# Gates of both token halves together, and four smaller edits, in a two-layer trunk on one core

## The chip, the cores and the metric

The program runs on one core of a Trainium2 chip. The metric is the device time of one execution in microseconds (us); three runs of the kernel before gave 1740.96, 1741.60 and 1741.65, median 1741.6. TensorE (PE) multiplies; PEld is its weight load; VectorE is DVE, ScalarE is ACT, GpSimd is POOL, and SyncE (SP) issues most DMAs.

## The reference

`x` is 1024 tokens by 1024 features in float32, `c` one vector that conditions every sub-layer through scale, shift and gate. Two layers; the change lies in the first, whose mixer is recurrent:

```python
for i in range(DEPTH):                                   # 2 layers
    mod = silu(c) @ w_mod[i] + b_mod[i]                  # six vectors of 1024
    sh_m, sc_m, gt_m, sh_f, sc_f, gt_f = split(mod, 6)
    h = rms_norm(x, norm_mix_g[i]) * (1 + sc_m) + sh_m
    y = recurrent_mixer(h) if i == 0 else pool_mixer(h)
    x = x + gt_m * y
    h = rms_norm(x, norm_ffn_g[i]) * (1 + sc_f) + sh_f
    x = x + gt_f * (square(relu(h @ w1)) @ w2)           # 4096 wide
return rms_norm(x, final_norm_g)

def recurrent_mixer(h):
    gate_branch = gelu(h @ w_y + b_y)
    xr = causal_depthwise_conv(h @ w_in + b_in)          # width 4
    r, g = sigmoid(xr @ w_a + b_a), sigmoid(xr @ w_x + b_x)   # 4 blocks of 256 x 256
    log_a = 8 * r * log_sigmoid(lam)
    a, u = exp(log_a), sqrt(-expm1(2 * log_a)) * (g * xr)
    s[t] = a[t] * s[t-1] + u[t]                          # scan over tokens
    return (s * gate_branch) @ w_out + b_out
```

## The kernel before

Features lie on the 128 partitions, tokens along the free axis: `x` is eight blocks of 128 features, and the tokens are two halves of `H` = 512 (h = 0, 1). Float32 products are made of three fp32r matmuls of 512 columns: `mm3` (L184) multiplies high by high, high by low and low by high parts, and `proj` (L192) sums eight blocks, 24 matmuls. High parts are copies by ACT, low parts subtractions by DVE (`split_part`, L178), by POOL, or a DMA that adds (`neg_part`, L160).

Resources: six accumulators of PSUM for products (`acc_mm`), two for small ones (`small_ps`), 19 slots of 4 x 512 columns, seven temporaries, and three raw buffers (`rawp`) that weight loads and the conditioning's loads share. A product can't begin until an accumulator has been evicted.

The order on each engine is not the order of the text. A planner runs the program on its own costs when it is built, and gives a free engine the ready instruction that was written first; the engines then keep that order and wait for each other by semaphores. `tc.issue_after` and the helper `after` (L321) tie an instruction behind another one on its engine by hand.

The first layer goes as follows.

- Start (L102 to L402). Loads of `x`, of the modulation weights `mw` and of the projection's weights `w_k`. `s0` sums the squares of half 0: ACT squares a block, DVE adds it (`SumSq.add`, L252). `rstd_bcast` (L265) sums over partitions by small matmuls with a column of ones (L272), takes root and reciprocal, and spreads the result over all partitions by two fp32r matmuls with diagonals (L286), high and low part. `scale_of(k)` and `bias_of(k)` (L335, L338) make the modulation's columns on DVE. Then eight steps k normalize a block and multiply it into six accumulators `ps6` (L401).
- Between (L408 to L470). Half 1 of `x` is loaded, its squares are summed (`s1`, L443), the six accumulators are evicted with the bias (`conv_input`, L446), blocks 6 and 7 of half 0 are projected, half 1 is normalized and projected, and `conv` does the four taps.
- Gates (L502 to L565). For each of four heads, `split_unit` loads and splits a gate unit and two gelu units, and then for each half: `gates` (four gate products of six matmuls, sigmoids, Exp, Tanh, Sqrt, the scan) and two `gelu_block` (24 matmuls each). The scan writes over the convolution's output; Exp has a temporary `a`.

```python
    for hd in range(4):
        rate[0] = hd
        ...
        for h in range(2):
            gates(hd, ug, h)
            if (hd, h) == (3, 1):
                split_y(0)
            for mi in range(2):
                gelu_block(2 * hd + mi, uy[mi], h)
```

- Conditioning. The remaining 80 columns of the modulation (`mod_steps`, L216) are a 512 KB load `mb` and a DVE instruction (L207) each. `split_unit` and `f2_weights` call `drip(n)`, which issues n of them; n is `rate[0]` in the mixer and `DRIPS` (1 each) in the FFN. The first FFN's norm needs 24 of them, its end 32.
- First FFN (`f1(0, 0)`, L858): the norm of half 1 (`ffn_norm`) is made beside the first products of half 0.
- End (L1013 to L1038). The last products come in pieces: half 0, then the tokens of half 1 in two pieces of 256. `last_chunk` sums squares as they come; each letter of its plan names a sum, and equal letters are added on DVE. The last piece's sum is spread over the partitions before the root (`rstd_row`, L993), so that root and reciprocal take 128 x 256 elements.

## Time and profile before

| | |
|---|---|
| median of three runs | 1741.6 us |
| the profiled execution | 1740.4 us |
| its span, first to last instruction | 1738.5 us |
| mean granted clock of TensorE | 0.994 |
| PE busy | 1690.5 us (97%), 7472 matmuls |
| DVE, ACT, POOL busy | 1358.9, 967.2, 492.3 us (78, 56, 28%) |
| moved by DMA | 187.33 MB, mean 108 GB/s |

All times within the execution are from the span's start. A busy time is the union of an engine's instructions. Matmuls follow each other faster than each one lasts, so a busy PE may still run below its rate: the number of matmuls in a window tells more. The granted clock is 1.00 at 2.4 GHz and 0.50 at 1.2 GHz; a window with both shows a mean. Waits are put down to the instruction that came last by the profile.

### The profile page before, as it was taken

Reading aid. Unit: us, or ns where it says so; the run is one execution under the profiler, and the core shown is the slowest. Engines: PE = TensorE matmul, PEld = TensorE weight load, DVE = VectorE, ACT = ScalarE, POOL = GpSimd, SP = SyncE. Lnnn points to the kernel's source line nnn. Section 1 sums busy time; section 2 is a strip of 40 time slices with the busy share of each in tenths; the row PEclk is TensorE's granted clock in tenths of the full one; section 3 lists DMA queues with packets and bytes.
Section 4 is the critical chain, followed back from the end, with each engine's and each line's share of the span. In section 5 each row is a group of like instructions: output and inputs, shape, how many; then the busy total and the mean of one; then the engine's idle time right before and its main releaser. Section 6 shows DMA issues by size and latency. Waiting matters only on the chain.

```text
span 1738.5 us, 20871 instructions
## 1 busy us (share of the span) xinstructions
PE 1690.5 (97%) x7472; PEld 1386.7 (80%) x7472; DVE 1358.9 (78%) x2115; ACT 967.2 (56%) x1660; POOL 492.3 (28%) x419
## 2 busy tenths in 40 slices
PE   6899999999999999999999999999999999999997
PEld 4687778877788888888888888888878787878787
DVE  7897867589898989897973898559696868687847
ACT  6588886555454454545457787745444454545432
POOL 2132343103241414151416333303140405041403
PEclk9999999999999999999999999999999999999999
DMA  9423425642423333332319888841111112120202
GB/s 337 168 93 104 143 85 162 143 119 83 136 72 123 95 99 109 96 117 89 123 37 198 202 192 179 190 118 61 49 59 39 61 38 70 39 69 29 80 6 97
DMA packets 63175, 187.33 MB, mean 108 GB/s; under 512 B 6752, under 2 KB 9184, under 8 KB 63072
## 3 DMA queue, kind: packets, MB, share of 16 engines
q1 hardware_dynamic: 47376, 157.43, 27.6%
q0 software_dynamic: 15696, 28.58, 9.9%
q8 instruction: 58, 0.95, 0.2%
q14 instruction: 45, 0.37, 0.1%
HBM read 181.79 MB, written 4.19 MB: 107 GB/s over the span
## 4 chain that ended last, share of the span: by engine, by line
PE 75%; DVE 10%; issue 3%; ACT 3%; DMA 2%; POOL 1%; DVEq 0%; ACTq 0%; POOLq 0%
PE mm L188 25%; PE mm L189 25%; PE mm L190 25%; DMA mb<-in_wmod 2%; DVE mb L207 1%; DVE xa L773 1%; DVE xb L773 1%; POOL xa L782 1%; DVE xcb L440 1%; DVE w_a_s L181 1%; ACT c L777 0%; DVE gate L530 0%; PE sm L272 0%; DVE w_y L181 0%; DVE w_s L181 0%
## 5 line engine op out<-in xcount | busy, mean ns | idle before, releaser
L188 PE MATMUL mm<-hh,w_w 128*128 128x512 f32 x1024 | 399.7, 390 | 0.9 <-DVE xa L773 0.9
L189 PE MATMUL mm<-hl,w_w 128*128 128x512 f32 x1024 | 399.3, 390 | 0.0
L190 PE MATMUL mm<-hh,w_w 128*128 128x512 f32 x1024 | 399.0, 390 | 0.0
L782 POOL TENSOR_TENSOR xb<-xb,c 128x512 f32<-128x512 f32 x104 | 150.0, 1442 | 625.4 <-ACT c L777 625.2
L188 PEld LDWEIGHTS mm<-hh,w_w 128*128 128x128 f32 x1024 | 192.6, 188 | 43.1 <-DVE xa L773 3.0
L190 PEld LDWEIGHTS mm<-hh,w_w 128*128 128x128 f32 x1024 | 192.6, 188 | 40.2
L189 PEld LDWEIGHTS mm<-hl,w_w 128*128 128x128 f32 x1024 | 192.5, 188 | 39.5
L782 POOL TENSOR_TENSOR xa<-xa,c 128x512 f32<-128x512 f32 x104 | 159.7, 1535 | 145.2 <-ACT c L777 145.2
L777 ACT ACTIVATE c<-c,mod 128x512 f32<-128x512 f32 x104 | 75.3, 724 | 202.6 <-DVE c L803 135.5
L623 ACT ACTIVATE relu<-mm 128x512 f32<-128x512 f32 x128 | 76.2, 596 | 144.7 <-PE mm L190 144.7
L207 DVE SCALAR_TENSOR_TENSOR mb<-mb,cond 128x1024 f32<-128x1024 f32 x80 | 114.5, 1434 | 47.9 <-DMA mb<-in_wmod 47.9
L773 DVE SCALAR_TENSOR_TENSOR xa<-mm,mod,xa 128x512 f32<-128x512 f32 x156 | 113.0, 742 | 25.8 <-POOL xa L782 25.8
L181 DVE TENSOR_TENSOR w_w<-raw_w,w_w 128x512 fp32r<-128x512 f32 x112 | 106.8, 962 | 12.4 <-ACT w_w L180 12.4
L165 POOL DMA_DIRECT2D w_w<-in_w x80 | 70.5, 900 | 151.0 <-ACT w_w L164 120.6
L613 DVE TENSOR_TENSOR u<-usq,u 128x512 fp32r<-128x512 f32 x102 | 70.2, 688 | 16.1 <-ACT u L612 15.8
L188 PE MATMUL mm<-u,w_a_a 128*128 128x512 f32 x200 | 79.1, 396 | 2.3 <-DVE xb L773 1.2
L188 PE MATMUL mm<-u,w_w 128*128 128x512 f32 (+1 forms) x224 | 80.9, 361 | 0.0
L189 PE MATMUL mm<-u,w_w 128*128 128x512 f32 (+1 forms) x224 | 80.5, 360 | 0.1
L190 PE MATMUL mm<-u,w_w 128*128 128x512 f32 (+1 forms) x224 | 80.4, 359 | 0.0
L180 ACT CAST w_w<-raw_w 128x512 fp32r<-128x512 f32 x112 | 65.1, 612 | 25.0 <-PE mm L190 17.3
L189 PE MATMUL mm<-u,w_a_a 128*128 128x512 f32 x200 | 78.0, 390 | 0.0
L190 PE MATMUL mm<-u,w_a_a 128*128 128x512 f32 x200 | 77.9, 389 | 0.0
(326 smaller groups left out, 4030.0 us busy)
## 6 DMA issues: line engine op xcount, KB each, us to landing
raw_w<-in_w SPq DMA_DIRECT2D x148, 512.0 KB, 3.5
mb<-in_wmod SPq DMA_DIRECT2D x80, 512.0 KB, 3.8
w_w<-in_w POOLq DMA_DIRECT2D x80, 256.0 KB, 5.5
mw<-in_wmod SPq DMA_DIRECT2D x16, 512.0 KB, 11.0
raw_in<-in_w_in SPq DMA_DIRECT2D x8, 512.0 KB, 7.0
raw_y<-in_w_y SPq DMA_DIRECT2D x8, 512.0 KB, 3.7
raw_o<-in_w_out SPq DMA_DIRECT2D x8, 512.0 KB, 4.2
outT<-o SPq DMA_DIRECT2D x12, 256.0 KB, 2.2
```

The costliest lines, as they stand in the source:

```text
L165: nc.gpsimd.dma_start(w[:, 1, 0:n], src, accum_op=ALU.add)
L180: S.copy(w[:, 0, 0:n], raw)
L181: (eng or V).tensor_sub(w[:, 1, 0:n], raw, w[:, 0, 0:n].bitcast(F32))
L188: PE.matmul(out=ps, lhsT=wh, rhs=rh, start=first, stop=False)
L189: PE.matmul(out=ps, lhsT=wh, rhs=rl, start=False, stop=False)
L190: PE.matmul(out=ps, lhsT=w[:, 1, c:c + P], rhs=rh, start=False, stop=last)
L207: V.scalar_tensor_tensor(raw, raw, 1.0, cond, op0=ALU.mult, op1=ALU.mult, accum_out=m[:, e:e + 1])
L613: eng.tensor_sub(u[n][:, 1, jj, :], src, u[n][:, 0, jj, :].bitcast(F32))
L623: S.activation(r, ps, AF.Relu)
L773: V.scalar_tensor_tensor(xb, ps, g[:, r + 4 * row:r + 4 * row + 1], xb, op0=ALU.mult, op1=ALU.add)
L777: S.activation(t, src, AF.Identity, scale=g[:, r + 4 * row:r + 4 * row + 1])
L782: G.tensor_add(xb, xb, t)
```

## The change

Five edits.

- First norm: a class `ColumnSums` squares each block on ACT and adds over partitions and blocks on PE at once (four small matmuls a block, all accumulating in one PSUM tile); DVE's additions go. `rstd_bcast` gets a form `quick`: the diagonal in float32, one matmul, no high and low parts. DVE's `scale_of(0)` is now issued behind the norm's diagonal.
- Evictions: the six `conv_input` of half 0 are written before the squares of half 1.
- Gates: `gates` takes both halves of a head, function by function; half 0's sigmoids go to a slot, Exp and the scan write over the convolution's output, and the product of input gate and convolution is made before Exp. Then come the four gelu blocks; `split_y(0)` follows the last head.
- Conditioning: the rates of the four heads are 1, 2, 2, 3 instead of 0, 1, 2, 3, and the four units of the first FFN block take none.
- End: the last piece's plan is VVVVVXYZ instead of VVVVVVVX, and its norm is `rstd_bcast(..., quick=True)`; `rstd_row` goes. In `rstd_bcast` the loops over sums and quarters change places.

```diff
@@ -248,6 +248,7 @@
             self.name, self.n, self.plan, self.room = name, n, plan, room
             self.parts = {}
             self.i = 0
+            self.ps = None
         def add(self, xb):
             who = self.plan[self.i]
@@ -262,18 +263,43 @@
                 S.activation(sq, xb, AF.Square)
                 return (G if who == "G" else V).tensor_add(a, a, sq)
-    def rstd_bcast(ss, trace=None):
+    class ColumnSums:
+        def __init__(self, n=H):
+            self.n, self.parts, self.i, self.ps = n, {}, 0, small_ps()
+        def add(self, xb):
+            sq = tmp("sq", self.n)
+            S.activation(sq, xb, AF.Square)
+            for q in range(self.n // P):
+                PE.matmul(out=self.ps[:, q:q + 1], lhsT=sq[:, q * P:(q + 1) * P], rhs=ones[:, 0:1],
+                          start=(self.i == 0 and q == 0), stop=(self.i == NB - 1), skip_group_check=True)
+            self.i += 1
+    def rstd_bcast(ss, trace=None, quick=False):
         nq = ss.n // P
         parts = list(ss.parts.values())
-        ps = small_ps()
-        for q in range(nq):
+        ps = ss.ps
+        if ps is None:
+            ps = small_ps()
             for pi, a in enumerate(parts):
-                PE.matmul(out=ps[:, q:q + 1], lhsT=a[:, q * P:(q + 1) * P], rhs=ones[:, 0:1],
-                          start=(pi == 0), stop=(pi == len(parts) - 1))
+                for q in range(nq):
+                    PE.matmul(out=ps[:, q:q + 1], lhsT=a[:, q * P:(q + 1) * P], rhs=ones[:, 0:1],
+                              start=(pi == 0 and q == 0), stop=(pi == len(parts) - 1), skip_group_check=True)
         r = mp.tile([P, 4], F32, tag="rstd", name="rstd", bufs=2)
         root = S.activation(r[:, 0:nq], ps[:, 0:nq], AF.Sqrt, bias=eps, scale=1.0 / D)
         V.reciprocal(r[:, 0:nq], r[:, 0:nq])
+        if quick:
+            bc = small_ps()[:, 0:ss.n]
+            dg = tmp("dg", ss.n)
+            last = V.tensor_mul(dg.rearrange("p (q i) -> p q i", i=P), ident[:, None, :].to_broadcast([P, nq, P]),
+                                r[:, 0:nq, None].to_broadcast([P, nq, P]))
+            PE.matmul(out=bc, lhsT=ones, rhs=dg, start=True, stop=True)
+            if trace is not None:
+                trace[S], trace[V] = root, last
+            return bc
         rh = mp.tile([P, 4], F32R, tag="rstdh", name="rstdh", bufs=2)[:, 0:nq]
         V.tensor_copy(rh, r[:, 0:nq])
@@ -304,10 +330,10 @@
         hh[h] = Blocks(f"hh{h}", F32R)
         hl[h] = Blocks(f"hl{h}", F32R)
-    s0 = SumSq("m00", plan="VVVVVVVV")
+    s0 = ColumnSums()
     for k in range(NB):
         with tc.issue_after(cond_copy[k >= 6].ins) if k in (4, 6) else nullcontext():
-            last = s0.add(x[0][:, k, :])
+            s0.add(x[0][:, k, :])
     a, b = const.tile([P, NB], F32, name="amix0"), mod_tile(0, 0)
@@ -338,9 +364,8 @@
     def scale_of(k):
         column(a, 1, k, vcol("gmix0", k), b1[:, k:k + 1])
-    tail_of[V] = last
+    bc0 = rstd_bcast(s0, tail_of, quick=True)
     scale_of(0)
-    bc0 = rstd_bcast(s0, tail_of)
     parts = []
@@ -440,11 +465,11 @@
                 V.scalar_tensor_tensor(o, xr[:, k:k + H], vcol(f"cw{k}", m), o,
                                        op0=ALU.mult, op1=ALU.add)
+    xr = [conv_input(m, ps6[m], 0) for m in range(6)]
+    taken = last_traced(S)
     s1 = SumSq("m01", plan="VVVVVVVV")
     for k in range(NB):
         s1.add(x[1][:, k, :])
-    xr = [conv_input(m, ps6[m], 0) for m in range(6)]
-    taken = last_traced(S)
     xr.append(conv_input(6, proj(uin[6], hh[0], hl[0]), 0))
     bc1 = rstd_bcast(s1)
     xr.append(conv_input(7, proj(uin[7], hh[0], hl[0]), 0))
@@ -499,45 +524,51 @@
     behind.close()
-    def gates(hd, unit, h):
-        xchl = slot("xchl", (2, 2, H), F32R)
-        xch, xcl = xchl[:, 0, :, :], xchl[:, 1, :, :]
-        src = xc[h][:, 2 * hd:2 * hd + 2, :]
-        S.copy(xch, src)
-        V.tensor_sub(xcl, src, xch.bitcast(F32))
-        rs, gs = [], []
-        for mi in range(2):
-            b = 2 * hd + mi
-            for g in range(2):
-                ps = acc_mm()
-                for k in range(2):
-                    mm3(ps, unit, ((g * 2 + k) * 2 + mi) * P, xch[:, k, :], xcl[:, k, :], k == 0, k == 1)
-                t = tmp("gate")
-                S.activation(t, ps, AF.Sigmoid, bias=vcol("ba" if g == 0 else "bx", b))
-                (rs if g == 0 else gs).append(t)
-        aa = []
-        for mi in range(2):
-            b = 2 * hd + mi
-            av = tmp("a")
-            S.activation(av, rs[mi], AF.Exp, scale=coef[:, b:b + 1])
-            S.activation(rs[mi], rs[mi], AF.Tanh, scale=ncoef[:, b:b + 1])
-            aa.append(av)
-        for mi in range(2):
+    def gates(hd, unit, halves):
+        xchl, rs, gs = {}, {}, {}
+        for h in halves:
+            xchl[h] = slot("xchl", (2, 2, H), F32R)
+            src = xc[h][:, 2 * hd:2 * hd + 2, :]
+            S.copy(xchl[h][:, 0, :, :], src)
+            V.tensor_sub(xchl[h][:, 1, :, :], src, xchl[h][:, 0, :, :].bitcast(F32))
+        for h in halves:
+            room = slot("gates") if h == 0 else None
+            for mi in range(2):
+                b = 2 * hd + mi
+                for g in range(2):
+                    ps = acc_mm()
+                    for k in range(2):
+                        mm3(ps, unit, ((g * 2 + k) * 2 + mi) * P, xchl[h][:, 0, k, :], xchl[h][:, 1, k, :],
+                            k == 0, k == 1)
+                    t = tmp("gate") if room is None else room[:, 2 * mi + g, :]
+                    S.activation(t, ps, AF.Sigmoid, bias=vcol("ba" if g == 0 else "bx", b))
+                    (rs if g == 0 else gs)[h, mi] = t
+        both = [(h, mi) for h in halves for mi in range(2)]
+        hs = {(h, mi): xc[h][:, 2 * hd + mi, :] for h, mi in both}
+        for at in both:
+            G.tensor_mul(gs[at], gs[at], hs[at])
+        for at in both:
+            b = 2 * hd + at[1]
+            S.activation(hs[at], rs[at], AF.Exp, scale=coef[:, b:b + 1])
+            S.activation(rs[at], rs[at], AF.Tanh, scale=ncoef[:, b:b + 1])
+        for at in both:
             e = tmp("asq")
-            G.tensor_mul(e, aa[mi], aa[mi])
-            V.scalar_tensor_tensor(rs[mi], e, 1.0, rs[mi], op0=ALU.add, op1=ALU.mult)
-        for mi in range(2):
-            b = 2 * hd + mi
-            S.activation(rs[mi], rs[mi], AF.Sqrt)
-            hs = xc[h][:, b, :]
-            G.tensor_mul(gs[mi], gs[mi], hs)
-            V.tensor_mul(gs[mi], gs[mi], rs[mi])
-            V.tensor_tensor_scan(hs, aa[mi], gs[mi], 0.0 if h == 0 else carry[:, b:b + 1],
+            G.tensor_mul(e, hs[at], hs[at])
+            V.scalar_tensor_tensor(rs[at], e, 1.0, rs[at], op0=ALU.add, op1=ALU.mult)
+        for at in both:
+            h, b = at[0], 2 * hd + at[1]
+            S.activation(rs[at], rs[at], AF.Sqrt)
+            V.tensor_mul(gs[at], gs[at], rs[at])
+            V.tensor_tensor_scan(hs[at], hs[at], gs[at], 0.0 if h == 0 else carry[:, b:b + 1],
                                  op0=ALU.mult, op1=ALU.add)
             if h == 0:
-                V.tensor_copy(carry[:, b:b + 1], hs[:, H - 1:H])
+                V.tensor_copy(carry[:, b:b + 1], hs[at][:, H - 1:H])
     def gelu_block(m, unit, h):
         ps = proj(unit, hh[h], hl[h])
@@ -554,15 +585,14 @@
             V.tensor_sub(yl[h][:, k, :], xc[h][:, k, :], yh[h][:, k, :].bitcast(F32))
     for hd in range(4):
-        rate[0] = hd
+        rate[0] = (1, 2, 2, 3)[hd]
         ug = split_unit(w_g[hd], f"g{hd}")
         uy = [split_unit(w_y[m], f"y{m}") for m in (2 * hd, 2 * hd + 1)]
+        gates(hd, ug, (0, 1))
         for h in range(2):
-            gates(hd, ug, h)
-            if (hd, h) == (3, 1):
-                split_y(0)
             for mi in range(2):
                 gelu_block(2 * hd + mi, uy[mi], h)
+    split_y(0)
     wo = [split_unit(w_out[m], f"o{m}", G, 0) for m in range(4)]
     split_y(1)
@@ -680,7 +710,7 @@
     DRIPS = (1, 1, 1, 1, 1, 1, 1, 1)
     def f1_jobs(i, c, eng=None):
-        return [partial(lambda j: split_unit(w1[i, c * 4 + j], f"w1_{i}_{c}_{j}", eng, DRIPS[j]), j) for j in range(4)]
+        return [partial(lambda j: split_unit(w1[i, c * 4 + j], f"w1_{i}_{c}_{j}", eng, 0 if (i, c) == (0, 0) else DRIPS[j]), j) for j in range(4)]
     def f2_jobs(i, c, eng=None):
         return [partial(lambda r: f2_weights(i, c, r, eng), r) for r in range(4)]
@@ -990,17 +1020,6 @@
     osrc = outT.rearrange("(b p) t -> p b t", p=P)
     units = [split_unit(w2[1, 7, dp], f"w2_1_7_{dp}") for dp in range(4)]
-    def rstd_row(ss):
-        parts = list(ss.parts.values())
-        ps = small_ps()[:, 0:ss.n]
-        for pi, a in enumerate(parts):
-            PE.matmul(out=ps, lhsT=ones, rhs=a, start=(pi == 0), stop=(pi == len(parts) - 1))
-        r = tmp("rrow", ss.n)
-        S.activation(r, ps, AF.Sqrt, bias=eps, scale=1.0 / D)
-        V.reciprocal(r, r)
-        return r
     def final_norm(bc, h, t0, n):
         per = H // n
         for k0 in range(0, NB, per):
@@ -1034,8 +1053,8 @@
     n1 = 256
     sa = last_chunk(0, 0, H, "VVVVVVVV")
     sb = last_chunk(1, 0, n1, "VVVVVVVV", once(lambda: final_norm(rstd_bcast(sa), 0, 0, H)))
-    sc = last_chunk(1, n1, H - n1, "VVVVVVVX", mid_norm())
-    final_norm(rstd_row(sc), 1, n1, H - n1)
+    sc = last_chunk(1, n1, H - n1, "VVVVVXYZ", mid_norm())
+    final_norm(rstd_bcast(sc, quick=True), 1, n1, H - n1)
 def _layout(inputs):
```

## Rows read from the trace of the kernel before

**Rows 1.** The page's slices of PE: busy tenths in 40 equal slices.
```profile
PE   6899999999999999999999999999999999999997
```

**Rows 2.** Waits of PE, whole span: us in total, times, longest us.
```profile
PE mm L188 <- ACT gelu L545: 6.1, 4, 1.9
...
PE mm L188 <- ACT xr L426: 4.0, 1, 4.0
...
PE sm L272 <- DVE mod L210: 3.9, 1, 3.9
```

**Rows 3.** Windows of PE: window, length, busy us (matmuls), granted clock, DMA share, GB/s.
```profile
60.00:70.00 10.00, 8.17 (x26) 0.66 0.07 28
...
230.00:240.00 10.00, 8.13 (x29) 0.83 0.37 132
240.00:250.00 10.00, 10.00 (x45) 1.00 0.08 31
...
360.00:370.00 10.00, 6.76 (x27) 0.83 0.48 155
```

**Rows 4.** ACT by line, 122 to 253: count | busy us, mean ns | idle before, releaser.
```profile
L517 ACT ACTIVATE gate<-mm,vec 128x512 f32<-128x512 f32 x28 | 17.6, 691 | 0.2
L524 ACT ACTIVATE a<-gate,coef 128x512 f32<-128x512 f32 x14 | 9.4, 716 | 0.1
...
L517 ACT ACT_TABLE_LOAD x7 | 9.0, 1283 | 0.1
...
L533 ACT ACTIVATE gate<-gate 128x512 f32<-128x512 f32 x14 | 8.7, 632 | 12.1 <-DVE gate L530 12.0
```

**Rows 5.** Window of all engines, 122 to 253 (PE, PEld, DVE, ACT, POOL busy).
```profile
122.00:253.00 131.00, 124.88 (x541) 101.87 (x540) 106.56 (x153) 108.71 (x147) 44.53 (x30) 0.99 0.36 117
```

**Rows 6.** Conditioning's columns by line, 122 to 262, columns as in rows 4.
```profile
L207 DVE SCALAR_TENSOR_TENSOR mb<-mb,cond 128x1024 f32<-128x1024 f32 x18 | 26.5, 1475 | 11.2 <-DMA mb<-in_wmod 11.2
```

**Rows 7.** Timeline of DVE, 345 to 365: start, duration, instruction [idle before <- releaser].
```profile
358.83 1.23 DVE L207 SCALAR_TENSOR_TENSOR mb<-mb,cond 128x1024 f32<-128x1024 f32 x1 [2.08 <-DMA mb<-in_wmod]
...
361.26 1.23 DVE L207 SCALAR_TENSOR_TENSOR mb<-mb,cond 128x1024 f32<-128x1024 f32 x1 [0.59 <-DMA mb<-in_wmod]
...
362.41 0.69 DVE L263 TENSOR_TENSOR ssq<-ssq,sq 128x512 f32<-128x512 f32 x1
```

**Rows 8.** Timeline of PE, 3 to 21 and about 70.
```profile
4.17 3.78 PE L154 MATMUL sm<-dg,ones 128*128 128x512 f32 x4 [4.17 <-DVE dg L152]
11.96 1.87 PE L272 MATMUL sm<-ones,ssqm00V 128*128 128x1 f32 x8 [4.01 <-DVE ssqm00V L263]
...
18.66 2.08 PE L401 MATMUL mm<-hh,w_k 128*128 128x512 f32 x4 [1.86 <-ACT hh L328]
...
69.97 0.95 PE L272 MATMUL sm<-ones,ssqm01V 128*128 128x1 f32 x8
```

**Rows 9.** Timeline of DVE, 10 to 20 and 45 to 52.
```profile
11.82 1.34 DVE L328 CUSTOM_DVE_ANT_0 mw<-mw,cond,bmix 128x1024 f32<-128x1024 f32 x1
...
15.26 0.68 DVE L284 TENSOR_TENSOR dg<-ident,rstd 128x512 fp32r<-128x512 f32 x1
...
47.20 1.34 DVE L328 CUSTOM_DVE_ANT_0 mw<-mw,cond,bmix 128x1024 f32<-128x1024 f32 x1 [1.26 <-DMA mw<-in_wmod]
```

**Rows 10.** Window of all engines, 40 to 60; last three: granted clock, DMA share, GB/s.
```profile
40.00:60.00 20.00, 17.27 (x75) 13.63 (x74) 14.40 (x31) 10.53 (x16) 1.76 (x2) 1.00 1.06 350
```

**Rows 11.** Timeline of all engines, the line of ACT's evictions.
```profile
61.11 3.56 ACT L426 ACTIVATE xr<-mm,vec 128x512 f32<-128x512 f32 x6
```

**Rows 12.** Timeline of DVE, 59 to 80: last addition, first normalized block of half 1.
```profile
61.90 0.69 DVE L263 TENSOR_TENSOR ssqm01V<-ssqm01V,sq 128x512 f32<-128x512 f32 x1
...
76.98 0.75 DVE L294 SCALAR_TENSOR_TENSOR nt<-xb,amix,sm 128x512 f32<-128x512 f32 x1
```

**Rows 13.** Timeline of DVE, 1724 to the end.
```profile
1726.80 0.69 DVE L263 TENSOR_TENSOR ssqo1256V<-ssqo1256V,sq 128x256 f32<-128x256 f32 x1 [0.48 <-ACT sq L262]
...
1729.69 1.75 DVE L1001 RECIPROCAL rrow<-rrow 128x256 f32<-128x256 f32 x1 [1.80 <-ACT rrow L1000]
```

## The prediction, made before the change was run

> **What bounds the kernel now.** I read the slices of the page first: TensorE (PE) is busy nine tenths or more almost everywhere, so the time is PE's stream of matmuls plus the holes in it [rows 1]. The holes are at the start (slices one and two) and at the end. Next the list of PE's waits, where three entries meet the change: the gelu evictions (6.1 us in four waits), the first eviction of the projection (4.0) and a column sum that is put down to `mod` (3.9) [rows 2]. Then windows of 10 us. An undisturbed one holds 45 matmuls of 512 columns, all at the granted clock 1.00. Three are short of that: 26, 29 and 27 matmuls [rows 3]. In them PE was partly idle, and the granted clock is 0.66, 0.83 and 0.83: it fell from the 2.4 GHz level to the 1.2 GHz level after the idle stretch. What that costs beside the idle time: 0.34 of 10 us, half the clock granted for 6.8 us, is 3.4 us of matmuls lost; 0.17 of 10 us is 1.7 us. So each of the change's parts is priced by the hole that it meets, with the clock loss behind it. FFN work after 430 us has no part in the change and I leave it as it is.
>
> **The gates (main part).** Per head PE has 2 x 4 gate products of 6 matmuls and 4 gelu products of 24: 144, at 45 in 10 us some 32 us. Before, PE does four gate products, two gelu products, and so on; with six accumulators the next product then needs a gelu eviction. ScalarE (ACT) can't give it: its queue has the square roots in front, and they waited 12.0 us for VectorE's (DVE) `gate` [rows 4]. That is the 6.1 us of [rows 2], and the last of these waits brought the clock loss of 1.7 us in the window 230 to 240 [rows 3].
> After, eight gate products come first (11 us of PE), then four gelu products (22 us), and the next head's gates want an accumulator held by gelu only about 24 us after the last gate product. ACT by then has to do 8 exponentials and hyperbolic tangents, two table loads, 4 roots and then the gelus: 8 x 0.71 + 2 x 1.28 + 4 x 0.63 = 10.8 us, plus the waits for the roots; even with 4 us for these it is there at 15. So all four waits go: 6.1 + 1.7 = 7.8 us. ACT's own load falls: four table loads a head for eight, 4 x 1.28 = 5.1 us of a head [rows 4]; that is off the path and I count it at nothing. The scans in place make Exp wait for GpSimd's (POOL) products; POOL has as many as before and was busy 44.5 of 131 us with 30 operations [rows 5], so nothing either; without that cover Exp is late by a POOL product or two, 1.5 us each, inside the 9 us of slack.
> Bounds: 7.8 gained, down to nothing gained (rivals below). Moving `split_y(0)` behind the gelus: its 16 copies and subtractions, 0.6 to 0.7 us each, have PE's last two gelu products (11 us) before they are wanted; nothing.
>
> **Conditioning.** The rates 1, 2, 2, 3 take 24 columns of the modulation in the mixer instead of 18: six more DVE instructions of 1.48 us in the mean, 9 us [rows 6], and six more DMAs of 512 KB past the weights in SP's queue. DVE is busy 106.6 of 131 us and waits 11.2 us for these very DMAs [rows 5, 6], which leaves 13 us: it just fits. What is queued behind such a wait is the whole of DVE's work, weights and gates. I count nothing and keep the overflow as a rival.
> What it buys: in the first FFN block no columns are left except one. There DVE stood 2.08 and 0.59 us for the DMA of `mb`, did 1.23 us each, and only then made the last sum `ssq` (362.41 to 363.10) [rows 7], for which PE's column sum in front of its queue waited 3.9 us [rows 2]; the label `mod` is DVE's next instruction. Clock loss behind it 1.7 [rows 3]. Without the two columns the sum is ready about 2.08 + 0.59 + 2 x 1.23 = 5.1 us sooner, more than the wait. One column of the next layer stays there, which may stand for its DMA as the second did (0.59). 3.9 + 1.7 - 0.6 = 5.0 us gained; bounds 5.6 and, if that one column waits as the first did, 3.9 - 2.1 = 1.8 and the clock loss not saved.
>
> **First norm.** DVE's seven additions go, and PE gets 64 small fp32 matmuls in place of 8. Eight of them took 1.87 us at the start and 0.95 us at 69.97 us, where the clock is granted in full [rows 8], so PE is at its lower level in the first 20 us. They queue behind the broadcast of the condition (4.17 + 3.78 = 7.95 us). Before, the eight were done at 13.8. After: at the low level throughout 7.95 + 8 x 1.87 = 22.9 us; at the high level 7.95 + 8 x 0.95 = 15.6. The rows show the clock rising only after PE had worked nearly without a break since 18.66 us; the new stream has no break from 4.17 on, but no row shows whether one-column matmuls raise it. I take 17: high for most of the stream.
> The Trainium skill ("TensorE: Matmul & The Clock Gate", LDWEIGHTS) says that a weight load costs its column count over 1.2 GHz however few columns are multiplied, 107 ns for 128; by that page 64 loads are, as an estimate, 6.8 us, and the stream would end at 14.8. The row of the start has 0.23 us a matmul, and the row decides.
> The quick broadcast saves a cast, a subtraction and a diagonal (0.68) on DVE, but `scale_of(0)`, 1.34 us, which ran at 11.82 under PE's column sum, now stands behind the norm on the path [rows 9]: 1.34 less 0.68 and two of some 0.2, plus 0.3. So the first projection starts 3.5 us later; bounds plus 2 and plus 9.
> Up to 58 us the DMA engines are the limit (share 1.06, 350 GB/s [rows 10]), and at 47.20 DVE stands 1.26 us for the last `mw` [rows 9]; that much is absorbed. The projection's end moves from 57.8 (PE's wait of 4.0 us behind it ended with the first eviction, at 61.8 [rows 2, 11]) to about 60.
>
> **Evictions first.** Before, ACT did eight squares of the second half and only then the six evictions (61.11 to 64.67), so PE stood 4.0 us and lost 3.4 us of clock [rows 2, 3, 11]. Ceiling 7.4. After, the squares stand behind the evictions (3.56 us), the last addition, at 62.59 before [rows 12], ends near 68 (the later projection included), and from the column sum (69.97) to the first normalized block (76.98, DVE) went 7.0 us [rows 8, 12]: 75 to 76 instead of 77. PE reaches the end of its two projections at 71 and waits there, with some clock lost. The whole of first norm and evictions: I take 1.5 us gained. Bounds: 7.4 gained if the norm's chain is short, 3 lost if the column sums stay at the low level (7.7 late at 58 us, of which the old hole and its clock take back 4 to 5).
>
> **End.** The last plan drops DVE's addition at 1726.80, behind which the last eviction stood (0.69 us at most, taken as 0.45), and the reciprocal of 256 columns (1.75 us) becomes one of two columns, against a diagonal, under 0.68, and one more product, about 0.4 (eight small ones took 0.95) [rows 8, 9, 13]: 0.45 + 1.75 - 0.68 - 0.4 = 1.1 us gained; bounds 0.4 and 1.5.
>
> **Sum.** 7.8 + 5.0 + 1.5 + 1.1 = 15.4. The profiled execution took 1740.4 us (span 1738.5 and 1.9 around it): 1725.0. The median of the runs is 1741.6, 1.2 above it: 1726.2 us.
>
> **Rivals.**
> *DVE becomes the bound of the mixer.* For it: 106.6 busy, plus 9, plus 11.2 x 24/18 = 15 of DMA waits is 130.6 us against the 123 that PE keeps of its 131 [rows 5, 6]. Against: PE needs DVE's results only a head later. Price: the overhang of 7.6 is paid at the mixer's end, 1726.2 + 7.6 = 1734.
> The Trainium skill ("SBUF — State Buffer", Who interferes with whom) speaks for this: a DVE instruction with two SBUF inputs and a GpSimd one that reads SBUF get in each other's way. The trace agrees (a column took 1.23 us in the FFN, where POOL multiplies nothing, and 1.48 in the mixer [rows 6, 7]), and POOL's eight products of a head now come in two runs.
> *Column sums at the low clock.* For it: the eight at 11.96 ran at that level. The term of 1.5 becomes minus 3: 1726.2 + 4.5 = 1731.
> *Table reloads (the slower side).* The gate products reach ACT one in 1.33 us (6 matmuls), a sigmoid is 0.69: the planner can fill the pause with an exponential, and each one costs two loads, 2.57 us [rows 4]. ACT's load of a head is about 108.7/131 x 32 - 5 = 22 us; it decides from 4 such pairs a head (10.3 us), where ACT passes PE's 32. At six, 22 + 15.4 is 5 us over in each of four heads: 20 us lost instead of 7.8 gained, 1754. Against: before, ACT never changed tables back within a phase (7 loads for the 7 sigmoid phases [rows 4], and as many for each of the three other kinds).
> *The planner hides little.* Only the waits of the gates go and the start loses 3: 1741.6 - 7.8 + 3 = 1737. For it: the squares and the column sums stand in an order that its own costs set, not the trace. Against: each hole has its own cause.
>
> **Numbers.** Forecast 0.52; DVE-bound 0.14; low clock 0.16; little gained 0.10; reloads 0.08. Range 1719 (evictions pay 7 instead of 1.5) to 1740. A difference under 0.2% (3.5 us) can't be told from none here. Faster: the first three and most of the fourth's better half, 0.83; same 0.08; slower 0.09.
>
> **What would show it.** Right: no wait of PE for `gelu` between 120 and 255 us, four table loads a head, no window at a granted clock under 1.00 near 235 and 365, the reciprocal of 1.75 us gone, PE's first projection matmul at 20 to 23 us. Wrong: more than 16 table loads in the gates, PE waiting for `w_g`, `xchl` or a sigmoid there, column sums of 1.87 us for each eight up to 22 us, or a new wait of PE between 63 and 78 us longer than 7 us.

## The result, and the profile after

The changed kernel takes 1761.0 us (median of four runs) against 1741.6: 1.0112 times the time before, 95% interval 1.0098 to 1.0125. It is slower by 19.4 us where 15.4 us less was forecast. (The ratio of `spread3_new`, below, leaves out one execution that took 7728 us.) The profiled execution took 1759.1 us, its span 1757.3. The spans differ by 18.8 us, and the starts of PE's matmuls say where:

| stretch (first matmul to first matmul) | before | after | difference |
|---|---|---|---|
| start to first `w_k` | 18.7 | 24.2 | +5.6 |
| `w_k` (to its last) | 38.3 | 39.5 | +1.2 |
| to the first `w_g` (projection, half-1 norm) | 65.8 | 65.0 | -0.8 |
| gates, `w_g` to first `w_o` | 139.5 | 155.5 | +16.0 |
| output projection | 88.5 | 88.5 | 0.0 |
| to the first product of the second FFN matrix | 50.7 | 47.4 | -3.2 |
| to the end of its last in the kernel | 1325.5 | 1325.9 | +0.4 |
| from there to the end | 11.7 | 11.2 | -0.5 |

**PE's waits and clock.** The slices of PE, answering to [rows 1]; the waits, to [rows 2]; windows (length, busy us, matmuls, granted clock, DMA share, GB/s), to [rows 3]:

```profile
PE   7898889999999999999999999999999999999998
```
```profile
PE mm L189 <- DVE xchl L538: 16.0, 5, 6.3
...
PE mm L188 <- ACT hh L321: 4.8, 1, 4.8
...
PE sm L312 <- DVE dg L310: 2.9, 3, 2.0
```
```profile
80.00:90.00 10.00, 6.42 (x21) 0.67 0.20 62
...
170.00:180.00 10.00, 6.60 (x18) 0.66 0.53 175
200.00:210.00 10.00, 5.24 (x20) 0.81 0.30 79
210.00:220.00 10.00, 10.00 (x40) 0.85 0.71 228
240.00:250.00 10.00, 3.68 (x17) 0.85 0.38 121
...
380.00:390.00 10.00, 7.97 (x35) 1.00 0.44 108
```

No wait for `gelu` is left, as forecast. In its place PE waits 16.0 us for `xchl`, the high and low parts of a head's input, 14.2 of it in heads 1 to 3. Behind the three longest of these waits the granted clock goes to the 1.2 GHz level: 17 to 20 matmuls where 45 fit. The low clock that stood near 365 us, at the FFN norm, is gone: that norm now stands near 384 us, and the window around it is at 1.00. A gates stage without any wait takes 130.6 us (`no_cols_old`, below). This one is 24.9 above it: 16.0 of waits, and the rest mostly the clock (an estimate from its records: 13.9 us of matmuls at half the rate, 7.0).

**The gates.** Columns as in [rows 4 to 6]; all engines from 128 to 284 us, ACT's table loads and the columns there:

```profile
128.00:284.00 156.00, 139.64 (x580) 112.90 (x579) 124.06 (x170) 126.49 (x171) 50.94 (x35) 0.93 0.37 118
```
```profile
L549 ACT ACT_TABLE_LOAD x8 | 10.3, 1283 | 0.1
L558 ACT ACT_TABLE_LOAD x8 | 10.3, 1283 | 4.0 <-DVE coef L523 3.8
L566 ACT ACT_TABLE_LOAD x8 | 10.3, 1283 | 0.1
L559 ACT ACT_TABLE_LOAD x4 | 5.1, 1283 | 0.1
L576 ACT ACT_TABLE_LOAD x4 | 5.1, 1283 | 0.1
```
```profile
L207 DVE SCALAR_TENSOR_TENSOR mb<-mb,cond 128x1024 f32<-128x1024 f32 x22 | 32.7, 1486 | 17.1 <-DMA mb<-in_wmod 17.0
```

32 table loads, eight a head and not four: the planner takes an Exp between the sigmoids and a Sqrt between the tanhs. DVE is busy 124 us, and 17 us more it stands for columns' transfers. Head 1 on DVE, the wait of PE that ends it, and the same head on ACT (start, duration, instruction [idle before <- releaser]):

```profile
181.92 1.23 DVE L207 SCALAR_TENSOR_TENSOR mb<-mb,cond 128x1024 f32<-128x1024 f32 x1 [3.39 <-DMA mb<-in_wmod]
...
183.39 2.00 DVE L207 SCALAR_TENSOR_TENSOR mb<-mb,cond 128x1024 f32<-128x1024 f32 x1 [0.24 <-DMA mb<-in_wmod]
...
189.63 1.23 DVE L207 SCALAR_TENSOR_TENSOR mb<-mb,cond 128x1024 f32<-128x1024 f32 x1 [2.80 <-DMA mb<-in_wmod]
...
194.75 1.23 DVE L207 SCALAR_TENSOR_TENSOR mb<-mb,cond 128x1024 f32<-128x1024 f32 x1 [2.07 <-DMA mb<-in_wmod]
...
202.43 1.28 DVE L568 TENSOR_TENSOR_SCAN xcb<-xcb,carry,gate 128x512 f32<-128x512 f32 x1
...
204.21 1.89 DVE L181 TENSOR_TENSOR w_y<-raw_y,w_y 128x512 fp32r<-128x512 f32 x3
...
207.22 1.22 DVE L538 TENSOR_TENSOR xchl<-xca,xchl 128x1024 fp32r<-128x1024 f32 x1
```
```profile
208.49 0.79 PE L189 MATMUL mm<-xchl,w_g 128*128 128x512 f32 x1 [4.50 <-DVE xchl L538]
```
```profile
197.73 0.63 ACT L566 ACTIVATE gate<-gate 128x512 f32<-128x512 f32 x1 [4.59 <-DVE gate L563]
...
202.38 1.05 ACT L537 CAST xchl<-xca 128x1024 fp32r<-128x1024 f32 x1
```

Read it downwards: DVE, in order, waits for three columns in the midst of the head's chain (the work from the sigmoids to the scans), so the last scan ends at 203.7; the roots on ACT wait for DVE, the gelus for the roots, the cast of `xchl` stands behind two gelus and three casts, and its subtraction, at 207.22, behind `w_y`'s. PE had ended the gelu products at 203; it issues the first gate matmul, which takes high parts alone, at 203.5, and the second only at 208.5.

**Start, half-1 norm, FFN norm, end.** PE's timeline at the start and at the column sum of half 1 (answers to [rows 8]); DVE's about 80 us [rows 12], 384 us [rows 7] and at the end [rows 13]:

```profile
4.16 3.78 PE L154 MATMUL sm<-dg,ones 128*128 128x512 f32 x4 [4.16 <-DVE dg L152]
8.18 10.77 PE L276 MATMUL sm<-ones,sq 128*128 128x1 f32 x64 [0.24 <-ACT cond L155]
20.32 2.07 PE L299 MATMUL sm<-dg,ones 128*128 128x512 f32 x2 [1.36 <-DVE dg L297]
24.23 2.08 PE L426 MATMUL mm<-hh,w_k 128*128 128x512 f32 x4 [1.84 <-ACT hh L354]
...
71.66 1.02 PE L289 MATMUL sm<-ones,ssqm01V 128*128 128x1 f32 x8 [0.25 <-DVE ssqm01V L264]
```
```profile
73.02 0.18 DVE L293 RECIPROCAL rstd<-rstd 128x4 f32<-128x4 f32 x1
...
77.95 4.09 DVE L465 SCALAR_TENSOR_TENSOR xca<-xr,vec,xca 128x512 f32<-128x512 f32 x3
...
82.04 0.73 DVE L320 SCALAR_TENSOR_TENSOR nt<-xb,amix,sm 128x512 f32<-128x512 f32 x1
```
```profile
382.53 1.22 DVE L207 SCALAR_TENSOR_TENSOR mb<-mb,cond 128x1024 f32<-128x1024 f32 x1 [2.19 <-DMA mb<-in_wmod]
```
```profile
1748.13 0.17 DVE L293 RECIPROCAL rstd<-rstd 128x2 f32<-128x2 f32 x1 [1.50 <-ACT rstd L292]
1748.33 0.93 DVE L297 TENSOR_TENSOR dg<-ident,rstd 128x256 f32<-128x256 f32 x1
```

### The profile page after: what moved, and what is told of

Same layout as the page of the kernel before. It is cut to its first block, busy times and chain, and to the rows that moved or that the text cites. A ratio compares the mean times of both kernels' runs of the same rounds, so it can differ in the third digit from the quotient of the medians.

```text
span 1757.3 us, 20983 instructions
## 1 busy us (share of the span) xinstructions
PE 1706.2 (97%) x7542; PEld 1399.9 (80%) x7542; DVE 1358.5 (77%) x2104; ACT 967.4 (55%) x1660; POOL 503.0 (29%) x419
## 4 chain that ended last, share of the span: by engine, by line
PE 77%; DVE 9%; DMA 3%; issue 2%; ACT 2%; POOL 1%; DVEq 0%; ACTq 0%; POOLq 0%; SPq 0%
PE mm L188 26%; PE mm L189 25%; PE mm L190 25%; DMA mb<-in_wmod 3%; DVE mb L207 1%; DVE xa L803 1%; DVE xb L803 1%; DVE xcb L465 0%; DVE w_y L181 0%; POOL xa L812 0%; PE sm L289 0%; DVE w_a_s L181 0%; DVE xcb L568 0%; DVE xca L568 0%; ACT c L807 0%
## 5 line engine op out<-in xcount | busy, mean ns | idle before, releaser
L643 DVE TENSOR_TENSOR u<-usq,u 128x512 fp32r<-128x512 f32 x102 | 70.2, 688 | 18.7 <-ACT u L642 18.3
```

Source lines behind the costliest of these rows:

```text
L643: eng.tensor_sub(u[n][:, 1, jj, :], src, u[n][:, 0, jj, :].bitcast(F32))
```

## The experiments

"Stage" is from the first `w_g` to the first `w_o` matmul of the profiled run; ratios are to the kernel before on the same chip (1740.6 to 1741.0 us there), with 95% intervals. Each stage comes from one execution. Two pairs of runs have the same gates and the same columns, and their stages are still 1.3 us (`g_undone`, `ecx`) and 2.3 us (the changed kernel, `n_undone`) apart, so a smaller difference can't be told from none. The planner orders the whole program anew for each kernel; an edit can move instructions that it doesn't name.

**1. Parts undone or alone.** `g_undone`: `gates` and its loop as before in the changed kernel, the rates kept.

```diff
-        gates(hd, ug, (0, 1))
         for h in range(2):
+            gates(hd, ug, h)
...
```

> The gates as in the kernel before (half by half), all other parts of the change kept, the new rates of columns too. Theory A (the second half's xchl of the next head is queued behind the gate chain and the gelu evictions of this head, and TensorE waits for it): the gates stage returns from 155.3 to about 139.5 us, so 1761 - 16 = 1745 us, with no wait of TensorE for xchl and the four waits for gelu back (6.1 us). Rival B (the six added columns of conditioning overload VectorE and the DMA queue in this stage): the stage stays at 150 us or more and the time at 1755 or more.

Measured: 1.0038 (1.0023 to 1.0052), 1747.4 us; stage 140.2 with 24 columns. The gelu waits are back:

```profile
PE mm L188 <- ACT gelu L570: 6.5, 3, 3.1
```

So 15.3 of the 16.0 us come with the new gates; six more columns alone cost the old ones 0.7, which is not told from none. `g_only`: the kernel before with the new `gates` and their loop, `rate[0] = hd`.

> The kernel before with only the new gates (both halves together, rates of columns 0, 1, 2, 3 as before). Theory A: 1741.6 + 13 to 17 = 1755 to 1759 us, with waits for xchl of 10 us or more in heads 1 to 3. Rival B: without the added columns the waits for xchl nearly go and the time is within 3 us of 1741.6.

Measured: 1.0059 (1.0042 to 1.0076), 1750.1 us; stage 147.8. Between the two theories: the new gates lose 8.3 us with the 18 columns of before, and in the new form six more cost another 7.7 (5.4 by `n_undone`), where in the old form they cost 0.7 (2.0 by `ecx`).

```profile
PE mm L189 <- DVE xchl L513: 11.6, 3, 7.0
```

`n_undone`: the first norm of before in the changed kernel.

```diff
-    s0 = ColumnSums()
+    s0 = SumSq("m00", plan="VVVVVVVV")
...
-            s0.add(x[0][:, k, :])
+            last = s0.add(x[0][:, k, :])
...
-    bc0 = rstd_bcast(s0, tail_of, quick=True)
+    tail_of[V] = last
     scale_of(0)
+    bc0 = rstd_bcast(s0, tail_of)
```

> The changed kernel with the first norm's sums and broadcast as in the kernel before, the rest kept. Theory A: the first projection matmul is back at 18.7 us from 24.2, the last at 57 from 63.8, and all of it comes through: 1761 - 6 = 1755 us (1753 to 1757). Rival C (the start's loss is swallowed later, by the half-1 norm or the conditioning's DMAs): 1759 to 1761 us.

Measured: 1.0071 (1.0056 to 1.0086), 0.41% or 7 us under the changed kernel's ratio; first projection matmul at 19.1, stage 153.2. As expected: the loss of the start comes through.

`ecx`: gates and first norm of before; evictions, conditioning and end new.

> The kernel before with only the evictions ahead of the half-1 squares, the conditioning's new spread and the new end; gates and first norm as before. From the stages of the runs so far: start 0 to -1, gates +0.7, the norm of the FFN -1.5 to -3.7, the end -0.3: 1736 to 1740 us against 1741. If the new first norm was worth something after all, not under 1741.

Measured: 1.0007 (0.9998 to 1.0016), 1742.2 us: worth nothing together. The forecast had 5.0 for the conditioning, 1.1 for the end, and 1.5 for the evictions after the first norm's loss, which this run doesn't have. From the last `w_k` to the first `w_g` it takes 66.7 us (before 65.8), the gates 141.5, the norm 49.6.

**2. Is it the place of `xchl`, the table loads, or the columns?** `xchl_early`: the next head's `xchl` is written ahead of this head's chain.

```diff
...
+        nxt = xchl_of(hd + 1) if hd < 3 else None
         both = [(h, mi) for h in halves for mi in range(2)]
```

> The changed kernel, with the next head's xchl (high and low parts of both halves) traced before this head's gate chain instead of after its gelus; no work is added or left out. Theory A: no wait of TensorE for xchl in heads 1 to 3 (16 us in all) and no low clock behind them (some 10 us): 1761 - 20 to 26 = 1735 to 1741 us. Rival B (VectorE is late because it waits for the columns' DMAs in the midst of the chain, wherever xchl stands): a wait for gelu or for an accumulator appears in its place and the time stays at 1752 or more.

Measured: 1.0105 (1.009 to 1.012), 1758.9 us. The waits for `xchl` are gone, but `w_g`'s low part, next behind the chain, is late in its place, and then `w_o`; stage 147.7, output projection 5.7 longer. Theory A has the right wait and the wrong cause: all that DVE makes for the next head is late.

```profile
PE mm L190 <- DVE w_g L181: 7.4, 3, 2.7
PE mm L190 <- POOL w_o L181: 3.7, 1, 3.7
```

`grouped`: ACT held to the written order (`sig` is the head's last sigmoid, `th` its last tanh); `early_grouped`: both edits.

```diff
+            with tc.issue_after(sig.ins):
                 S.activation(hs[at], rs[at], AF.Exp, scale=coef[:, b:b + 1])
...
+            with tc.issue_after(th.ins):
                 S.activation(rs[at], rs[at], AF.Sqrt)
```

> The changed kernel with ScalarE held to the order in which the gates are written: the exponentials and tanhs of a head behind its last sigmoid, the square roots behind its last tanh, so four table loads a head in place of eight. No work is added or left out. Theory D (the planner's order splits the functions again, and the four extra loads of 1.28 us lengthen each head's chain, behind which xchl and w_g of the next head stand): 16 loads go, each head's chain is some 5 us shorter, the waits for xchl fall from 16 to under 5 us: 1761 - 12 to 20 = 1741 to 1749 us. Rival B (VectorE's waits for the columns' DMAs set the length of the chain): the loads go and the waits for xchl stay above 10 us: 1755 us or more.

> Both the early xchl and the held order. Theory D: as the held order alone or a little better, 1738 to 1748 us; w_g and xchl no longer late, at most 3 us of waits in heads 1 to 3. Rival B: 1753 us or more.

Measured: 1.0076 (1.006 to 1.0092) and 1.0087 (1.0072 to 1.0101); stages 149.8 and 152.5. 16 table loads (20.5 us of ACT) less give back 5.7 us of the stage, and waits for `xchl` of 11.4 us stay: rival B's side. With both edits PE waits for `gelu` instead:

```profile
PE mm L188 <- ACT gelu L585: 15.4, 3, 7.2
```

`no_cols`:

```diff
-        rate[0] = (1, 2, 2, 3)[hd]
+        rate[0] = 0
```

> The changed kernel with no conditioning columns in the gates stage; they are all made right behind it, so only the stage from the first w_g to the first w_o matmul is read (139.5 us before, 155.5 after). Theory D: 145 us or more, since the order on ScalarE is the same and the next head's xchl stands behind the chain as before. Rival B: 140 us or less.

Measured: stage 133.3. Theory D falls: with the same 32 table loads and the same order only 1.8 us of waits are left once DVE has no columns; DVE is busy 89 of 133.5 us.

```profile
PE mm L189 <- DVE xchl L538: 1.8, 3, 1.5
```
```profile
130.00:263.50 133.50, 131.65 (x578) 108.06 (x577) 89.06 (x118) 123.71 (x166) 46.13 (x35) 1.00 0.14 44
```

**3. The columns' waits or their work?** In the gates only, `cols_res` reads `cond` in place of a transferred block, and `cols_light` transfers it and multiplies 8 elements (`n = 8`).

```diff
-                nc.sync.dma_start(raw, wmod[i, j, e])
-                mod_column(m, e, raw)
+                V.scalar_tensor_tensor(raw, cond, 1.0, cond, op0=ALU.mult, op1=ALU.mult, accum_out=m[:, e:e + 1])
```
```diff
-                mod_column(m, e, raw)
+                V.scalar_tensor_tensor(raw[:, 0:n], raw[:, 0:n], 1.0, cond[:, 0:n], op0=ALU.mult, op1=ALU.mult, accum_out=m[:, e:e + 1])
```

> The changed kernel whose 24 columns in the gates stage are computed from a vector already in SBUF: their 512 KB transfers are left out, so the conditioning values are not the model's; VectorE's instructions stay. Read is the stage from the first w_g to the first w_o matmul (139.5 us before, 155.5 after, 133.3 without columns). Theory W (VectorE is held, in order, by columns that wait for their transfers: 17 us of such waits): 134 to 139 us. Theory V (the 1.2 to 2.3 us that each column takes on VectorE fill it): 147 us or more.

> The changed kernel whose columns in the gates stage keep their transfers but multiply only 8 of 1024 elements, so the conditioning values are not the model's; VectorE is spared some 30 us and still waits in order for each transfer. Same stage. Theory W: 148 us or more. Theory V: 134 to 139 us.

Measured: stages 143.0 and 145.0. Neither theory alone: without transfers 12.5 us come back, without work 10.5, without both 22.2 (`no_cols`). Whether the transfers cost by DVE's waits alone, or also in the queue and the raw buffers that they share with the weights, was not taken apart. In `cols_light` DVE stands 40.6 us for transfers:

```profile
L224 DVE SCALAR_TENSOR_TENSOR mb<-mb,cond 128x8 f32<-128x8 f32 x23 | 7.6, 331 | 40.6 <-DMA mb<-in_wmod 40.6
```

**4. Columns elsewhere.** `spread` has the first norm of before; `spread_q` adds `quick=True` to its `rstd_bcast`.

```diff
-        rate[0] = (1, 2, 2, 3)[hd]
+        rate[0] = (1, 1, 1, 0)[hd]
...
                 if m0 == 0:
-                    drip(1)
+                    drip(2)
```

> The new gates, evictions and end, the first norm as before, and the conditioning's columns spread otherwise: 9 instead of 24 in the gates stage (1, 1, 1, 0 a weight load), two instead of one behind each of the first eight blocks of the output projection, where VectorE is idle half the time. Theory W or V: gates stage 134 to 138 us, the output projection 88.5 to 91, the rest as without the new first norm: 1735 to 1739 us against 1741. If the new gates lose by their own order (theory A or D), the stage stays over 143 and the time over 1743.

> The same with the short broadcast of the first norm (one multiplication by the diagonal in full fp32 in place of two in halves), the sums still added on VectorE. If the short broadcast is what the new first norm loses by, the first projection matmul comes some 1 us or more later than without it; if the 64 one-column matmuls are, it comes within 0.5 us of 18.7 and the time within 1 us of the kernel above.

Measured: 1.0064 (1.0048 to 1.0079) and 1.0066 (1.0054 to 1.0078): a miss. The stage is 138.0 and 138.5, but the output projection takes 102.0 and 97.8: the second four `w_o` wait behind the added columns.

```profile
PE mm L190 <- DMA w_o<-in_w_out: 8.9, 1, 8.9
```

The first projection matmul comes at 18.7 and 19.1, so the short broadcast costs 0.3. In the changed kernel the column sums end at 18.95 instead of 13.83: 5.1 of its 5.6 us are the 64 matmuls. The chain behind them is 0.5 longer, with `scale_of(0)` in it, which `spread_q` leaves in its old place.

`spread2` moves the second lot behind those loads, with the evictions of before; `spread2_grouped` is held to the written order too, `spread2_old` has the old gates; `no_cols_old` is the old gates without columns.

```diff
                 if m0 == 0:
                     drip(1)
+                elif h == 0:
+                    drip(2)
```

> The new gates and the new end, the first norm and the order of its evictions as before; 9 columns in the gates stage, one behind each of the first eight blocks of the output projection and two behind each of the four blocks of its second four rows' first half, where the loads of w_o are already out. Gates stage 136 to 138 us, output projection 88.5 (no wait for w_o's transfers), 47 to 50 to the second FFN matrix: 1734 to 1739 us against 1741. If the columns collide there with the weights of the first FFN block, its stage grows by what the stage of the gates saved: 1740 to 1743.

> The same with ScalarE held to the written order (four table loads a head). The 16 loads less were worth 5.7 us of the stage with 24 columns; with 9 columns the waits for xchl are down to about 4 us, so at most that: 0 to 4 us faster than without.

> The same spread of columns with the gates half by half as before. If the new gates are worth what they remove (the waits for gelu, 6.1 us, and the low clock behind one, 1.7) once VectorE has room, this is 4 to 8 us slower than with the new gates; if the spread alone removes the waits for gelu, the two are within 2 us.

> The gates half by half as before with no columns in their stage (made right behind it, so only the stage from the first w_g to the first w_o matmul is read; 133.3 us with the new gates). If the waits for gelu come from the change of functions on ScalarE, the stage is 138 to 140 us; if they come from columns on VectorE, it is 131 to 134.

Measured: 1.0018 (1.0005 to 1.0031), 1.0000 (0.9991 to 1.0009), 0.9998 (0.999 to 1.0007). Stages 141.1, 140.4, 139.8: all three wait 6.8 us for `xchl` in head 0, where DVE still has convolutions and now three columns. The columns are not enough to explain it: `spread` has the same three there and waits 0.7, and its planner's order has the first subtraction for `xchl` at 123.1 us behind two low parts of `w_y`, where `spread2_old` has it at 128.3 behind four. The held order is worth 0.7 here, less than can be told from none. The output projection is back at 88.5 to 88.7. And `no_cols_old` has a stage of 130.6 with no wait in it at all, and ACT's roots wait 1.3 us for DVE's `gate` instead of 12.0 [rows 4], with the table loads as before: the waits for `gelu` in the kernel before came from columns, not from the change of functions.

```profile
124.40:254.90 130.50, 130.50 (x577) 108.09 (x576) 83.80 (x114) 121.14 (x162) 43.91 (x36) 1.00 0.14 45
```
```profile
L559 ACT ACTIVATE gate<-gate 128x512 f32<-128x512 f32 x16 | 9.8, 630 | 1.5 <-DVE gate L556 1.3
```

`spread3_old` and `spread3_new` differ in the gates alone: none of the nine columns in head 0, and the first FFN block takes its columns as before.

```diff
-        rate[0] = (1, 1, 1, 0)[hd]
+        rate[0] = min(hd, 1)
...
-        ... 0 if (i, c) == (0, 0) else DRIPS[j] ...
+        ... DRIPS[j] ...
```

> The kernel before (its gates, first norm and evictions), with the new end and its columns moved: none in head 0, one a weight load in heads 1 to 3 (9 in the gates stage in place of 18), 8 in the first half of the output projection as before, two behind each of the first four blocks of its second half. If columns on VectorE are what makes the gates wait, the stage is 131 to 135 us (139.5 before, 130.6 without columns) with at most one wait for gelu, and the time 1729 to 1735 us against 1741. If the table changes are, the stage is 138 or more and the time 1738 to 1742.

> The same with the new gates. Without columns they took 133.3 us against 130.6 of the old ones, with 24 columns 153 to 155 against 140: they leave VectorE less room, so 2 to 6 us slower than the kernel above: 1732 to 1740 us.

Measured: stages 133.1 (two waits for `gelu`, 1.9 us) and 137.1, as expected; whole 1.0035 (1.0023 to 1.0047) and 1.0046 (1.0032 to 1.006), a miss, since the output projection takes 99 to 100 us: PE waits there for DVE's sums. They differ from `spread2` in the heads that take the columns and in the four columns with the first FFN block's weights; which of the two costs it was not taken apart by a run. The trace of `spread3_old` points at the four: two of them stand on DVE 69.4 and 74.2 us into the output projection, behind 1.6 and 3.0 us of waiting for their transfers, and PE's wait of 8.8 us ends at 79.7; `spread2_old` has no column between 64 and 90 us.

```profile
PE sm L289 <- DVE ssq L264: 13.1, 2, 8.8
```

No run beats the kernel before. Not tried: `spread3_old` with the first FFN block free of columns, as in `spread2_old`. From the stretches of these two, 18.8 + 38.3 + 65.2 + 133.1 + 88.5 + 46.6 + 1328.0 + 11.5 + 1.8 around the span, an estimate is 1732 us, if those four columns are what the output projection loses by.

The stage by columns that the rates put there:

| columns | 0 | 9, none in head 0 | 9, three in head 0 | 18, none in head 0 | 24, three in head 0 |
|---|---|---|---|---|---|
| old gates | 130.6 | 133.1 | 139.8 | 139.5 | 140.2, 141.5 |
| new gates | 133.3 | 137.1 | 138.0, 138.5, 141.1 | 147.8 | 155.5, 153.2 |

Where the columns stand counts as well as how many there are: nine with three in head 0 take the old gates as long as 18 without.

## Why the prediction was wrong

**Gates: 7.8 gained; measured 16.0 lost. The step that failed** is "the next head's gates want an accumulator held by gelu only about 24 us after the last gate product", from which "So all four waits go: 6.1 + 1.7 = 7.8 us" was taken. The waits went. But PE's next gates want more than an accumulator: `xchl` and `w_g`, which DVE makes behind the chain. The text said of the rival "PE needs DVE's results only a head later"; it needs them as soon as the gelus are through. In the old form a half's chain is half as long and PE has two gelu products behind each; in the new one the chain of four blocks stands in one piece and the next head's work behind it. That picture is read from the traces; shown by runs is that the new gates take 2.7 us more without columns, 4.0 with nine in heads 1 to 3, 8.3 with 18, and 11.7 and 15.3 with 24, in runs that differ in the gates alone. The hole that I priced was also not what it seemed: the roots on ACT waited 12.0 us for DVE's `gate` [rows 4], and I stopped there instead of asking what DVE had in front of `gate`. It was the columns (`no_cols_old`).

**Six more columns at nothing ("it just fits"): wrong.** They cost 5.4 to 7.7 us in the new gates, 0.7 to 2.0 in the old. Busy time plus waits, 106.6 + 11.2 of 131 [rows 5, 6], was an average; waits in order hit inside the chain. The rival "DVE becomes the bound" named the engine, but had an overhang paid once at the mixer's end, at 7.6 us in place of some 24 (gates and columns, 7.8 forecast to 16.0 lost); the waits come in each head. The other rival's table pairs came only in part: 32 loads, as many as before, so "four table loads a head" is wrong. 16 fewer are worth 5.7 us of the stage with 24 columns; without columns all 32 leave 1.8 us of waits. Two of the forecast's own signs of being wrong came true: more than 16 table loads, and PE waiting for `xchl`.

**First norm: 3.5 us later forecast, 5.6 measured**, and 8.5 to 9.5 in the seven other profiled executions that have it: the 64 matmuls went 8.2 to 19.0 us here and take 13.8 us where the clock stays low (below). My 17 for their end was earlier than any of the eight, 18.95 to 22.9; the bound of plus 9 was the usual case. At 47 us little or nothing was absorbed: the `w_k` stretch is 1.2 us longer here, and at most 0.6 shorter in the other seven. 7 of the 19 us are this term (`n_undone`).

**Evictions with it: 1.5 gained forecast,** a number that was taken and not added up; measured, with the first norm, 6.0 later at the first `w_g`. The ceiling of 7.4 counts 0.7 twice: the low clock began at 60.5 us, while PE was idle until 61.8. The hole at 61.8 is gone (first `w_in` at 64.4, right behind `w_k`), and a new one of 4.8 us stands at 83.6 with the low clock behind it. From the column sum (71.66) to the first normalized block (82.04) it went 10.4 us, where 7.0 were taken over from before: the convolutions, ready sooner, stand on DVE ahead of it. With the first norm of before, five runs with the new order take 66.3 to 67.2 us from the last `w_k` to the first `w_g`, seven with the old one 64.8 to 65.8: about 1.4 lost. (With the new first norm all eight have the new order and take 65.0 to 66.3.)

**FFN norm: 5.0 gained forecast, 3.2 measured.** The remaining column waited 2.19 us, the bound that I gave, where I took 0.59; the low clock went. That is the better case: in `g_undone`, `ecx`, `grouped` and `early_grouped`, with the same edit, a low clock stays behind the norm, and the stretch takes 49.2 to 49.8, so 0.9 to 1.5 gained. **End: 1.1 forecast, 0.5 measured**: the diagonal took 0.93 and not under 0.68. The old end took 11.4 in `g_only`, and the new one 10.7 to 11.7 elsewhere, so this term is not told from none.

**Range.** Its lower end, 1719, doesn't follow from its own reason: 7 in place of 1.5 gives 1720.7. The measured time lies 21 us above its upper end; apart from the table rival, at 1754, no line of the forecast has the gates get slower.

## What to carry to other kernels

Before grouping work to save waits, list everything that the bottleneck engine's next block needs and who makes it behind the grouped chain; a wait named after one engine (ACT's gelu) may be caused by another's queue (columns on DVE), and taking those away is the test. Work that waits for transfers on an in-order engine costs its wait where it stands, so place it by the queue around it, not by the engine's mean load.

## What was not expected of the hardware

PE's clock during one-column matmuls. In the changed kernel it was granted in full for a while and fell to the 1.2 GHz level while PE issued them without a break (windows of line 276):

```profile
8.40:11.40 3.00, 3.00 (x29) 1.00 1.03 413
12.00:18.00 6.00, 6.00 (x30) 0.50 1.05 402
```

From one start to the next that is 0.11 and 0.21 us. In `g_undone` the same window shows the clock at 1.00 with the same slow matmuls, and all 64 take 13.8 us (so in six other runs that have them):

```profile
12.00:18.00 6.00, 6.00 (x29) 1.00 1.05 404
```
```profile
8.63 13.81 PE L276 MATMUL sm<-ones,sq 128*128 128x1 f32 x64 [0.74 <-ACT cond L155]
```

The first clock record of `g_undone` stands at 32.7 us, where its matmuls of 512 columns go from 0.43 to 0.23 us from start to start; before it the profile shows 1.00. So near the start the granted clock can't be read without the matmuls' own spacing. The Trainium skill ("TensorE: Matmul & The Clock Gate", Seeing it yourself) warns that the clock's trace events can be unreliable; this trace shows no wrong event, only a stretch without one. The Trainium skill's rule for a weight load ("TensorE: Matmul & The Clock Gate", LDWEIGHTS), its columns over 1.2 GHz, cited in the prediction, gives 107 ns for 128 columns, as an estimate. It agrees with the spacing at the full clock (0.11 us) and not with that at the low one (0.21).

DVE beside POOL. The column at 183.39, which began while POOL multiplied, took 2.00 us; the one at 181.92, which began 0.36 us before POOL's multiplication, took 1.23. In the kernel before, the 48 columns that no multiplication on POOL overlapped took 1.21 to 1.23 us each, and others up to 2.32. The forecast's "in the FFN, where POOL multiplies nothing" holds for the columns of [rows 7] alone.

```profile
182.28 2.02 POOL L554 TENSOR_TENSOR gate<-gate,xcb 128x512 f32<-128x512 f32 x1 [0.23 <-ACT gate L549]
184.32 1.97 POOL L562 TENSOR_TENSOR asq<-xca 128x512 f32<-128x512 f32 x1
```
